# Larger, ordered first transfers and an indexer rotation that swaps halves by DMA, in a two-layer sparse-attention and recurrence trunk

## The chip, the cores and the metric

One core of one Trainium2 chip runs the whole program in one launch. The metric is the device time of that launch in microseconds (us); less is better. The time before is the median of three runs; the profile is of one more execution, with its own time.

## The reference, cut to what matters

Two layers over 256 tokens of width 1024, all in float32. The change touches the indexer, which decides for every query which 64 keys it keeps, and the very first loads.

```
h = rmsnorm(x)
q, k, v, ga, iq, ik, iw, xr, gr, ma, mb = split(h @ w_in)      # iq: 16 heads of 64, ik: one head of 64
iq, ik = rope(iq), rope(ik)          # rope: [x1*c - x2*s, x2*c + x1*s], x1 and x2 the halves (32 + 32)
score[t, s] = sum_h iw[t, h] * relu(iq[t, h] . ik[s])          # causal, the 64 best s per t are kept
attn = softmax over the kept keys (q, k, v);   y_a = (attn * silu(ga)) @ w_out_attn
hr = rg_lru(conv(xr));                         y_b = (hr * silu(gr)) @ w_out_rnn
x = x + (sigmoid(ma)*y_a + sigmoid(mb)*y_b) @ w_o
```

## The kernel before, in words

**Layout.** Activations stand transposed: features on the 128 partitions, the 256 tokens in the free dimension. Every float32 matrix product is made of three fp32r matmuls: weights and activations are each split in a high part (a copy that rounds to fp32r) and a low part (the rest), and high x high, low x high and high x low add up in PSUM. All weights are one stream of 128x128 blocks, eight to a chunk of 512 KB, in the order of use. `Stream` (L528) loads a chunk into `raw` (4 buffers), and makes `wh` by a copy on ACT or DVE (L480, L482) and `wl` by a subtraction on DVE (L486; 6 buffers each). The first two chunks are "halved" (`HALVED`, L1237): they come as four loads of 256 KB into `rah` and become `whh` and `whl`.

**Order of the work.** `plan` (L65) lists the units of a layer: `head` (the indexer's key and weights `pk`, and its first three query blocks `iq`), then the other `iq` blocks, the recurrence (`xr`, `gr`, `gate`), the gates (`ga`, `ma`, `mb`), `q`, `k`, `v` and attention, and the output products. The units record operations; `Program.issue` (L285) then fixes the order on every engine before anything runs. It is a list scheduler: TensorE's work has its place in the units' order as priority, every other operation a due time that is counted back from the matmul that needs it, or from the next user of its buffer (L371). Costs and latencies are constants: a gathering DMA counts 300 ns for each transfer in it, and 2000 ns pass until it has landed (L227, L993). On each engine the instructions then run in exactly that order; one that waits holds up all behind it. All DMAs are issued by one queue, SyncE's (SP).

**The start.** L605 to L620 issue the first loads: half a chunk of weights, `head` (the norm gains, four table columns and the first block of x), the second block of x, more halves and chunks, three pairs of x blocks (`xp`), the positions and the parameters. In the fast memory x is one array in which a partition's eight blocks of 1 KB stand side by side. `scaled` (L766) splits x times the gain into `xg`, high and low; `Norm` sums the squares.

**The indexer.** `head` (L812) and `queries` (L856) rotate. `rotate` (L776) lets ACT copy the PSUM bank to `sw` in pieces of 32 partitions, each from the other half of its group of 64 (four ACT instructions for 128 partitions), while DVE multiplies the PSUM bank by the cosines; two more DVE instructions finish. For a query pair of 128 partitions (two heads of 64) two stacks `iqs` of 128 partitions are then built, each with the high part of one head on 64 partitions and its low part on the other 64, by two copies and two subtractions over 64 partitions each (L860 to L867). For the key, `kh` and `kl` hold the same 64 rows twice, also by two copies and two subtractions. `dots` (L874) multiplies the stacks by `kh` and `kl`; its matmuls get a priority 40 us later than their place (`LATE_DOTS`, L1246). ACT's relu makes `rl`, DVE adds it into the scores `wk`, and `select` (L901) finds the 64 best.

**Buffers that matter.** `iqr`, `sw`, `rl` and other work tiles share the five buffers of `f2`; PSUM has four banks `pp` for projections, two `pq` for dots and logits, two `pt`. `gather` (L978) already moves rows of `xs` between partitions by DMA, for the recurrence's block-diagonal gates, into tiles `xk` and `xf`.

Of the kernel before, what the change touches and what calls it, by code (L numbers as in the profile page):

```python
# [11 lines left out]
F32 = mybir.dt.float32  # L12
# [196 lines left out]
def real(a):  # L209
    return a.ap() if isinstance(a, V) else a  # L210
# [222 lines left out]
def trunk(ctx, tc, xT, pos, pre, par, fgb, wst, out):  # L433
# [15 lines left out]
    def const(s, shape, dt=F32, bufs=1, tag=None):  # L449
        return pg.tile(cp, tag or s, [P] + shape, dt, nm(s), bufs)  # L450

    def r2(s):
        return pg.tile(rp, "r2", [P, 2, T], F32R, nm(s), R2)
# [4 lines left out]
    def f2(s):  # L458
        return pg.tile(fp, "f2", [P, 2, T], F32, nm(s), F2)

    def f1(s):
        return pg.tile(fp, "f1", [P, T], F32, nm(s), F1)
# [2 lines left out]
        return pg.tile(pp, pool, [P, 2, T], F32, nm(s), {"pp": 4, "pq": 2, "pt": 2}[pool])  # L465


    def act(o, i, func, **kw):
        c = (50 if i.psum() else 94) + 0.833 * o.size() + (200 if "accum_out" in kw else 0)
        aps = [kw[k] for k in ("scale", "bias") if isinstance(kw.get(k), V)]  # L470
        outs = [o] + ([kw["accum_out"]] if "accum_out" in kw else [])
        pg.op("act", c + 93 * len(aps), outs, [i] + aps,
              lambda: nc.scalar.activation(real(o), real(i), func, **{k: real(v) for k, v in kw.items()}),
              TABS.get(func))

    def copy(o, i):

        n = o.size()
        pg.op("act", (50 if i.psum() else 94) + 0.833 * n, [o], [i],
              lambda: nc.scalar.activation(real(o), real(i), AF.Copy),  # L480
              alt=(67 + 1.046 * n if i.psum() else 69 + 0.52 * n,
                   lambda: nc.vector.tensor_copy(real(o), real(i))))  # L482
# [11 lines left out]
    def sub(o, a, b):  # L494
        tt(OP.subtract, o, a, b)
# [21 lines left out]
    def load(o, src, cost, beside=False):  # L517

        pg.op("dma", cost, [o], [], lambda: nc.sync.dma_start(real(o), src), beside=beside)
# [8 lines left out]
    class Stream:  # L528
# [6 lines left out]
        def load(self, upto):  # L535
            while self.nload < min(upto, NCH):
                c = self.nload
                self.nload += 1
                if c < HALVED:
                    self.raws[c] = []  # L540
                    for i in range(2):
                        raw = r2f("rah").join()
                        load(raw, wst[c][:, 512 * i:512 * i + 512], 800)
                        self.raws[c].append(raw)
                        yield
                    continue
                raw = pg.tile(wp, "raw", [P, 1024], F32, nm("raw"), RAWS)
                load(raw, wst[c], 1550)
                self.raws[c] = raw
                yield  # L550

        def chunk(self, c):
            if c not in self.parts:
                for _ in self.load(c + 1):
                    pass
                raw = self.raws.pop(c)
                pg.shift = -LEAD
                if c < HALVED:
                    self.parts[c] = []
                    for q in raw:  # L560
                        t = r2("whh").join(), r2("whl").join()
                        split(t, q)
                        self.parts[c].append(t)
                    pg.shift = 0.0
                    return self.parts[c]
                wh = pg.tile(wp, "wh", [P, 1024], F32R, nm("wh"), WBUF)
                wl = pg.tile(wp, "wl", [P, 1024], F32R, nm("wl"), WBUF)
                copy(wh, raw)
                sub(wl, raw, wh.bitcast(F32))
                pg.shift = 0.0  # L570
                self.parts[c] = (wh, wl)
            return self.parts[c]
# [26 lines left out]
    ws = Stream()  # L599
    prm = const("prm", [NPAR - NPRE])  # L600
    head = const("head", [NPRE + 2 * T])
    xp = [head[:, NPRE:].split(2)] + [const(f"xp{i}", [2, T]) for i in range(1, KD // 2)]
    x = [xp[k // 2][:, k % 2, :] for k in range(KD)]
    posi = const("posi", [T], I32)
    first = ws.load(KD // 2)  # L605
    load(head[:, :NPRE + T], pre, 400)
    next(first)
    load(x[1], xT[:, 1, :], 400, True)
    pg.shift = -9000.0
    load(posi, pos, 400)  # L610
    pg.shift = 0.0
    next(first)
    for i in range(1, KD // 2):
        load(xp[i], xT[:, 2 * i:2 * i + 2, :], 800)
        next(first)
        if i < HALVED:
            next(first)
    for _ in first:
        pass
    load(prm, par, 400)  # L620

    def pc(n, i=0):
        i += PC[n]
# [142 lines left out]
    def scaled(l, k):  # L766
# [6 lines left out]
        stt(t[1], xk, g, t[0].bitcast(F32), OP.mult, OP.subtract)  # L773
        return t

    def rotate(o, ps, sw, tabs, step):  # L776

        n = o.shape[0]
        for b in range(0, n, step):
            act(sw[b:b + step], ps[b ^ step:(b ^ step) + step], AF.Copy)  # L780
        mul(o, ps, tabs[0])
        mul(sw, sw, tabs[1])
        add(o, o, sw)
# [4 lines left out]
    class Layer:  # L788
# [23 lines left out]
        def head(self):  # L812

            pk, one, two = bank("pp", "pk"), bank("pp", "iq"), bank("pp", "iq")
            ps = pk[:, 0, :]
            self.R = R = self.norm.finish()
            for k in range(KD):
                for n, o in enumerate((ps, one[:, 0, :], one[:, 1, :], two[:, 0, :])):
                    mm3(o, self.xg[k], k == 0 and n != 2, k == KD - 1, True)
            ci, si = const("ci", [T]), const("si", [T])  # L820
            mul(ci, tab["i"][0], R)
            mul(si, tab["i"][1], R)
            self.ti = (ci, si)
            ikr, iwt = f1("ikr"), f1("iwt")
            rotate(ikr[:64], ps[:64], f1("sw")[:64], [t[:64] for t in self.ti], 32)
            mul(iwt, ps, R)
            kh, kl = self.kh, self.kl
            for b in (0, 64):
                copy(kh[b:b + 64], ikr[:64])
            for b in (0, 64):  # L830
                sub(kl[b:b + 64], ikr[:64], kh.bitcast(F32)[:64])
            pw = bank("pt", "iwps")
            pg.late = LATE_TURN
            for t in range(2):
                trans(pw[:, 0, t * P:t * P + P], iwt[:, t * P:t * P + P])
            pg.late = 0.0
            act(self.iwq, pw[:, 0, :].split(2)[:, :, 64:80], AF.Copy, scale=1.0 / 32.0)
            for k in range(0, KD, 2):
                self.make_h(k)
            self.banks["iq"] = one  # L840
            self.queries(1)
            self.banks["iq"] = two
# [13 lines left out]
        def queries(self, i):  # L856

            iqr = f2("iqr")
            rotate(iqr, self.banks["iq"], f2("sw"), [t.twice() for t in self.ti], 32)
            st = [r2("iqs") for _ in range(2)]  # L860
            for a in range(2):
                s = slice(64 * a, 64 * a + 64)
                copy(st[a][s], iqr[s])
            for a in range(2):
                s = slice(64 * a, 64 * a + 64)
                d = slice(64 - 64 * a, 128 - 64 * a)
                sub(st[a][d], iqr[s], st[a].bitcast(F32)[s])  # L867
            for n in range(2):
                for t in range(2):
                    self.dots(i - 1 + n, [st[a][:, n, :] for a in range(2)], t)  # L870
            if i == 7:
                self.select()
# [105 lines left out]
        def gather(self, kind, rows):  # L978

            parts = stretches(rows)  # L980
            src = {i: self.xs[i] for _, i, _, _ in parts}
            moves = []
            if kind == "plain":
                dst = r2("xf")
                for d, i, a, z in parts:
                    moves.append((dst[d:d + z - a], src[i][a:z]))
            else:
                dst = pg.tile(fp, "f1", [P, T], F32R, nm("xk"), F1)
                for h in range(2):
                    for d, i, a, z in parts:  # L990
                        d += h * len(rows)
                        moves.append((dst[d:d + z - a], src[i][a:z, h, :]))
            pg.op("dma", 300 * len(moves), [dst], list(src.values()),  # L993
                  lambda: [nc.sync.dma_start(real(o.bitcast(F32)), real(i.bitcast(F32))) for o, i in moves][-1])
            return dst

        def gate(self, j):
# [279 lines left out]
def layout(x, positions, norm_g, w_in, conv_w, conv_b, w_rg, b_rg, w_ig, b_ig, lru_lambda, w_out_attn, w_out_rnn,  # L1277
# [4 lines left out]
    def cols(v):  # L1282
        return v.reshape(-1, P).T
# [4 lines left out]
    sgn_a = np.where(p < 64, -1.0, 1.0).astype(np.float32)  # L1288
    sgn_i = np.where(p % 64 < 32, -1.0, 1.0).astype(np.float32)
    cw = conv_w.reshape(L, 4, KR, P).transpose(0, 2, 1, 3)  # L1290
    pre = np.concatenate([cols(norm_g), inv_a[:, None], sgn_a[:, None], inv_i[:, None], sgn_i[:, None], xT[:, 0]], 1)
    assert pre.shape == (P, NPRE + T)
    par = np.concatenate([cols(cw), cols(conv_b), cols(b_rg), cols(b_ig), cols(lru_lambda)], 1)
    assert par.shape == (P, NPAR - NPRE)
    fgb = np.ascontiguousarray(np.broadcast_to(final_g[None, :], (P, D)))
# [25 lines left out]
```

## Time and profile before

| | before |
|---|---|
| median of 3 runs | 707.88 us (706.57 to 708.32) |
| the profiled execution's own time | 706.28 us |
| its span in the profile | 704.5 us |
| TensorE (PE) busy | 687.6 us, 98% |
| VectorE (DVE) busy | 602.8 us, 86% |
| ScalarE (ACT) busy | 478.0 us, 68% |

How to read it: the span is the stretch that the profiler covers, 1.8 us less than the execution's time. A busy share is an average over stages; what an engine could still give is seen in the stretches and in the waits. "a <- b" in a row of instructions means that a is written from b; in brackets stands the idle time of the engine before an instruction and what ended it. For a matmul the time between two starts counts, not its duration, since matmuls overlap.

### The profile page before, as it was taken

The numbers are of one execution on the slowest core, as the hardware profiler recorded it, in microseconds if no ns is written. First come the engines' busy times: TensorE is split into PE (matmuls) and PEld (weight loads), VectorE is DVE, ScalarE is ACT, GpSimd is POOL, SyncE is SP. The second block draws the span as 40 slices with busy tenths as digits, with TensorE's granted clock in tenths as the row PEclk, the third lists the DMA queues.
The fourth block names the chain that finished last, engine by engine and source line by source line (L and its number), as shares of the span: only waits on it lengthen the run. The fifth ranks groups of instructions, "written<-read, shape, count | busy, mean of one in ns | idle before, by whom it ended". The sixth has DMA issues, their size and how long they took to land.

```text
span 704.5 us, 12625 instructions
## 1 busy us (share of the span) xinstructions
PE 687.6 (98%) x4720; PEld 638.4 (91%) x4720; DVE 602.8 (86%) x1179; ACT 478.0 (68%) x771; POOL 6.5 (1%) x18
## 2 busy tenths in 40 slices
PE   6999999999999999999999999999999999999996
PEld 5988999999999998888999899999999898988885
DVE  6989999999898959857779997999989987796573
ACT  7897675798895748544558866588769765773433
POOL 0000000000000000000000000000000000000000
PEclk9999999999999999999999999999999999999999
DMA  8545556666756452655553655566655554535521
GB/s 280 181 155 189 201 187 205 201 205 198 225 176 200 151 182 87 199 172 185 170 180 113 195 192 179 160 222 202 213 207 180 189 182 169 180 98 172 197 73 60
DMA packets 38536, 125.24 MB, mean 178 GB/s; under 512 B 4940, under 2 KB 7564, under 8 KB 38476
## 3 DMA queue, kind: packets, MB, share of 16 engines
q1 hardware_dynamic: 38476, 124.44, 54.1%
q8 instruction: 37, 0.61, 0.3%
q14 instruction: 23, 0.19, 0.1%
HBM read 119.77 MB, written 1.05 MB: 171 GB/s over the span
## 4 chain that ended last, share of the span: by engine, by line
PE 88%; ACT 5%; DVE 3%; issue 2%; DMA 1%; SPq 0%; DVEq 0%
PE rps L512 16%; PE yb L512 9%; PE q L512 7%; PE k L512 7%; PE ops L512 6%; PE ma L512 6%; PE ya L512 6%; PE v L512 6%; PE ga L512 6%; PE mb L512 5%; PE gps L512 5%; PE iq L512 3%; PE dots L512 2%; PE lg L512 2%; PE av L512 2%
## 5 line engine op out<-in xcount | busy, mean ns | idle before, releaser
L486 DVE TENSOR_TENSOR wl<-raw,wh 128x1024 fp32r<-128x1024 f32 x223 | 271.8, 1221 | 57.3 <-ACT wh L480 55.8
L480 ACT ACTIVATE wh<-raw 128x1024 fp32r<-128x1024 f32 x195 | 206.2, 1058 | 142.5 <-PE rps L512 21.9
L512 PE MATMUL rps<-hh,wh 128*128 128x256 f32 x352 | 99.7, 283 | 0.0
L512 PE MATMUL rps<-hl,wh 128*128 128x256 f32 x352 | 99.6, 283 | 0.0
L512 PE MATMUL rps<-hh,wl 128*128 128x256 f32 x352 | 99.6, 283 | 0.0
L512 PEld LDWEIGHTS rps<-hh,wh 128*128 128x128 f32 x352 | 67.4, 192 | 0.6 <-issue 0.4
L512 PEld LDWEIGHTS rps<-hh,wl 128*128 128x128 f32 x352 | 67.4, 191 | 0.2
L512 PEld LDWEIGHTS rps<-hl,wh 128*128 128x128 f32 x352 | 67.4, 191 | 0.0
L512 PE MATMUL yb<-wh,g 128*128 128x512 f32 x176 | 58.9, 396 | 0.0
L512 PE MATMUL iq<-xg,wh 128*128 128x256 f32 x232 | 45.7, 286 | 0.0
L512 PE MATMUL ya<-wh,aT 128*128 128x512 f32 x128 | 40.8, 396 | 0.0
L512 PEld LDWEIGHTS iq<-xg,wh 128*128 128x128 f32 x232 | 37.5, 192 | 0.0
L512 PEld LDWEIGHTS yb<-wh,g 128*128 128x128 f32 x176 | 32.5, 188 | 5.3
L512 PE MATMUL ga<-hh,wh 128*128 128x256 f32 x128 | 36.4, 284 | 0.8 <-DVE iwt L486 0.5
L512 PE MATMUL q<-hh,wl 128*128 128x256 f32 x128 | 36.4, 284 | 0.0
L512 PE MATMUL q<-hh,wh 128*128 128x256 f32 x128 | 36.4, 284 | 0.0
L512 PE MATMUL k<-hh,wl 128*128 128x256 f32 x128 | 36.3, 284 | 0.0
L512 PE MATMUL ga<-hl,wh 128*128 128x256 f32 x128 | 36.3, 283 | 0.0
L512 PE MATMUL q<-hl,wh 128*128 128x256 f32 x128 | 36.2, 283 | 0.0
L512 PE MATMUL k<-hl,wh 128*128 128x256 f32 x128 | 36.2, 283 | 0.0
L512 PE MATMUL k<-hh,wh 128*128 128x256 f32 x128 | 36.2, 283 | 0.0
L512 PE MATMUL ga<-hh,wl 128*128 128x256 f32 x128 | 36.2, 283 | 0.0
(254 smaller groups left out, 1945.4 us busy)
## 6 DMA issues: line engine op xcount, KB each, us to landing
raw<-in_wst_dram SPq DMA_DIRECT2D x223, 512.0 KB, 3.5
xk<-xs SPq DMA_DIRECT2D x24, 48.0 KB, 3.2
rah<-in_wst_dram SPq DMA_DIRECT2D x4, 256.0 KB
out_dram<-z SPq DMA_DIRECT2D x4, 256.0 KB, 2.3
xp<-in_xT_dram SPq DMA_DIRECT2D x3, 256.0 KB
fg<-in_fgb_dram SPq DMA_DIRECT2D x2, 256.0 KB
xk<-xs SPq DMA_DIRECT2D x8, 40.0 KB
xf<-xs SPq DMA_DIRECT2D x2, 160.0 KB
```

The source lines that it names most:

```text
L480: lambda: nc.scalar.activation(real(o), real(i), AF.Copy),
L486: lambda: nc.vector.tensor_tensor(real(o), real(a), real(b), op=op))
L512: lambda: nc.tensor.matmul(real(o), real(w), real(m), start=start, stop=stop, skip_group_check=grp))
```

## The change

It does two things. **First loads:** `head` takes the second block of x too (266 KB in place of 138), the last four blocks of x come as one load of 512 KB (`rest`), and the second weight chunk as one load of 512 KB into `raw`, its halves still being split one by one; only the first chunk is loaded in halves. The loads' order is written out: `head`, the two halves of chunk 0, `xp`, chunk 1, `rest`, chunks 2 and 3, positions, parameters. In memory, the first two blocks of x are part of `pre`, and the other six stand side by side for each partition.

**Rotation:** `rotate32` takes the place of `rotate` for the indexer (q and k of the attention keep the old one). ACT copies the whole bank to `o` in one instruction; a `move` of DMAs, one for each 32 partitions, writes the swapped halves to `sw`; then DVE multiplies `o` and `sw` by the tables and adds. The stacks: one split over all 128 partitions gives `one` (high) and `low`; a move of two DMAs fills `two` with the high and low rows of the second head, and then a move of one DMA overwrites the lower half of `one` with the low rows of the first. For the key, one split of 64 partitions and a move of two DMAs that doubles `kh` and `kl`. In the scheduler a move counts 250 ns for each of its DMAs, and the 2000 ns until it has landed; the existing gather uses the same function, and so counts 250 in place of 300.

```
-                if c < HALVED:
+                if c == 0:
...
-                    for q in raw:
+                    for q in raw if c == 0 else (raw[:, :512], raw[:, 512:]):
...
-    xp = [head[:, NPRE:].split(2)] + [const(f"xp{i}", [2, T]) for i in range(1, KD // 2)]
+    rest = const("xr", [4 * T])
+    xp = [head[:, NPRE:].split(2), const("xp", [2, T]), rest[:, :2 * T].split(2), rest[:, 2 * T:].split(2)]
...
-    load(head[:, :NPRE + T], pre, 400)
-    next(first)
-    load(x[1], xT[:, 1, :], 400, True)
-    pg.shift = -9000.0
-    load(posi, pos, 400)
-    pg.shift = 0.0
-    next(first)
-    for i in range(1, KD // 2):
-        load(xp[i], xT[:, 2 * i:2 * i + 2, :], 800)
-        next(first)
-        if i < HALVED:
-            next(first)
-    for _ in first:
-        pass
-    load(prm, par, 400)
+    def weights():
+        for _ in range(2 if ws.nload == 0 else 1):
+            next(first)
+
+    for n, f in enumerate((lambda: load(head, pre, 800), weights, lambda: load(xp[1].join(), xT[:, :2 * T], 800),
+                           weights, lambda: load(rest, xT[:, 2 * T:], 1550), weights, weights,
+                           lambda: load(posi, pos, 400), lambda: load(prm, par, 400))):
+        pg.shift = -1e6 + 1e4 * n
+        f()
...
+    def move(moves):
+
+        outs, ins = ({a.h: a for a in side}.values() for side in zip(*moves))
+        pg.op("dma", 250 * len(moves), list(outs), list(ins),
+              lambda: [nc.sync.dma_start(real(o.bitcast(F32)), real(i.bitcast(F32))) for o, i in moves][-1])
+
+    def rotate32(o, ps, sw, tabs):
+
+        n = o.shape[0]
+        act(o, ps, AF.Copy, also=(sw,))
+        move([(sw[b:b + 32], o[b ^ 32:(b ^ 32) + 32]) for b in range(0, n, 32)])
+        mul(o, o, tabs[0])
+        mul(sw, sw, tabs[1])
+        add(o, o, sw)
...
-            rotate(ikr[:64], ps[:64], f1("sw")[:64], [t[:64] for t in self.ti], 32)
+            rotate32(ikr[:64], ps[:64], f1("sw")[:64], [t[:64] for t in self.ti])
...
-            for b in (0, 64):
-                copy(kh[b:b + 64], ikr[:64])
-            for b in (0, 64):
-                sub(kl[b:b + 64], ikr[:64], kh.bitcast(F32)[:64])
+            split((kh[:64], kl[:64]), ikr[:64])
+            move([(t[64:], t[:64]) for t in (kh, kl)])
...
-            rotate(iqr, self.banks["iq"], f2("sw"), [t.twice() for t in self.ti], 32)
-            st = [r2("iqs") for _ in range(2)]
-            for a in range(2):
-                s = slice(64 * a, 64 * a + 64)
-                copy(st[a][s], iqr[s])
-            for a in range(2):
-                s = slice(64 * a, 64 * a + 64)
-                d = slice(64 - 64 * a, 128 - 64 * a)
-                sub(st[a][d], iqr[s], st[a].bitcast(F32)[s])
+            rotate32(iqr, self.banks["iq"], f2("sw"), [t.twice() for t in self.ti])
+            one, low, two = r2("iqs"), r2("iql"), r2("iqs")
+            split((one, low), iqr)
+            move([(two[:64], one[64:]), (two[64:], low[64:])])
+            move([(one[64:], low[:64])])
+            st = one, two
...
-            pg.op("dma", 300 * len(moves), [dst], list(src.values()),
-                  lambda: [nc.sync.dma_start(real(o.bitcast(F32)), real(i.bitcast(F32))) for o, i in moves][-1])
+            move(moves)
```

## Rows read from the trace of the kernel before

**Rows 1.** The page: busy time of each engine over the span.
```profile
PE 687.6 (98%) x4720; PEld 638.4 (91%) x4720; DVE 602.8 (86%) x1179; ACT 478.0 (68%) x771; POOL 6.5 (1%) x18
```

**Rows 2.** Busy time by stretch: PE, PEld, DVE, ACT, POOL, clock, DMA share, GB/s.
```profile
0.00:5.00 5.00, 0.16 (x1) 0.16 (x1) 0.76 (x4) 2.51 (x4) 1.28 (x10) 1.00 0.58 124
5.00:9.00 4.00, 3.85 (x15) 3.22 (x16) 1.71 (x5) 2.17 (x4) 0.00 (x0) 1.00 0.86 279
9.00:12.00 3.00, 2.95 (x23) 2.58 (x22) 2.65 (x6) 2.35 (x4) 0.00 (x0) 1.00 1.05 412
12.00:16.00 4.00, 2.34 (x17) 2.14 (x18) 3.96 (x8) 4.00 (x9) 0.00 (x0) 1.00 1.04 396
20.00:62.00 42.00, 39.00 (x292) 36.59 (x293) 38.50 (x63) 37.26 (x56) 0.00 (x0) 1.00 0.52 167
62.00:375.00 313.00, 313.00 (x2191) 292.98 (x2190) 273.16 (x559) 210.46 (x341) 2.65 (x4) 1.00 0.57 184
400.00:440.00 40.00, 38.89 (x300) 37.36 (x299) 35.93 (x71) 25.26 (x44) 0.32 (x1) 1.00 0.61 193
440.00:680.00 240.00, 240.00 (x1588) 220.31 (x1587) 206.95 (x411) 159.51 (x261) 2.27 (x4) 1.00 0.55 179
```

**Rows 3.** Who PE waited for over the whole span: total us, times, longest.
```profile
PE mb L512 <- DVE ga L486: 1.3, 1, 1.3
PE dots L512 <- ACT rl L473: 1.1, 1, 1.1
...
PE dots L512 <- DVE kl L486: 0.8, 1, 0.8
...
PE ga L512 <- DVE iwt L486: 0.5, 1, 0.5
```

**Rows 4.** Timeline, first 16 us: start, duration, instruction, idle before it.
```profile
4.84 0.58 PE L512 MATMUL pk<-xg,whh 128*128 128x256 f32 x1 [4.84 <-ACT xg L771]
...
5.71 0.51 ACT L771 ACTIVATE xg<-head 128x256 fp32r<-128x256 f32 x1 [0.92 <-DMA head<-in_xT_dram]
...
7.28 0.63 ACT L480 ACTIVATE whh<-rah 128x512 fp32r<-128x512 f32 x1 [1.06 <-DMA rah<-in_wst_dram]
...
14.27 0.38 PE L512 MATMUL pk<-xg,whl 128*128 128x256 f32 x1 [0.94 <-DVE whl L486]
...
15.44 0.28 PE L512 MATMUL pk<-xg,wh 128*128 128x256 f32 x1
...
15.56 0.28 PE L512 MATMUL pk<-xg,wl 128*128 128x256 f32 x1
```

**Rows 5.** ACT's instructions in 20 to 80 us by form: count, busy us, mean ns.
```profile
L473 ACT ACTIVATE sw<-iq 32x512 f32<-32x512 f32 x16 | 9.4, 590 | 0.3
L480 ACT ACTIVATE iqs<-iqr 64x512 fp32r<-64x512 f32 x7 | 4.4, 629 | 0.2
...
L480 ACT ACTIVATE kh<-ikr 64x256 fp32r<-64x256 f32 x2 | 0.8, 418 | 1.1 <-DVE ikr L486 1.1
```

**Rows 6.** DVE's instructions in 20 to 80 us by form.
```profile
L486 DVE TENSOR_TENSOR iqs<-iqr,iqs 64x512 fp32r<-64x512 f32 x8 | 5.5, 686 | 3.3 <-ACT iqs L480 3.1
...
L486 DVE TENSOR_TENSOR kl<-ikr,kh 64x256 fp32r<-64x256 f32 x2 | 0.8, 416 | 0.0
```

**Rows 7.** Timeline: the last query block's last matmul, its bank's product, `kl`'s last subtraction.
```profile
44.08 0.28 PE L512 MATMUL iq<-xg,wh 128*128 128x256 f32 x1
...
56.39 0.68 DVE L486 TENSOR_TENSOR iqr<-iq,ci 128x512 f32<-128x512 f32 x1
...
60.03 0.42 DVE L486 TENSOR_TENSOR kl<-ikr,kh 64x256 fp32r<-64x256 f32 x1
```

**Rows 8.** The tile `xk` of the existing gather: issue ns min/median/max, and landing.
```profile
L994 SPq DMA_DIRECT2D xk<-xs x64: 519/586/1311, 77.1 to 518.4; - x64
...
DMA to landing us min/median/max: 3.0/3.2/3.4
```

**Rows 9.** What the DMA queue (SP) waited for, 20 to 110 us.
```profile
SPq L519 <- DVE wl L486: 59.3, 22, 4.8
```

More of the change, by code (lines that the diff above doesn't have):

```diff
@@ L465, in bank, with act @@
         return pg.tile(pp, pool, [P, 2, T], F32, nm(s), {"pp": 4, "pq": 2, "pt": 2}[pool])
-    def act(o, i, func, **kw):
+    def act(o, i, func, also=(), **kw):
         c = (50 if i.psum() else 94) + 0.833 * o.size() + (200 if "accum_out" in kw else 0)
         aps = [kw[k] for k in ("scale", "bias") if isinstance(kw.get(k), V)]
-        outs = [o] + ([kw["accum_out"]] if "accum_out" in kw else [])
+        outs = [o, *also] + ([kw["accum_out"]] if "accum_out" in kw else [])
         pg.op("act", c + 93 * len(aps), outs, [i] + aps,
@@ L1290, in layout @@
     cw = conv_w.reshape(L, 4, KR, P).transpose(0, 2, 1, 3)
-    pre = np.concatenate([cols(norm_g), inv_a[:, None], sgn_a[:, None], inv_i[:, None], sgn_i[:, None], xT[:, 0]], 1)
-    assert pre.shape == (P, NPRE + T)
+    pre = np.concatenate([cols(norm_g), inv_a[:, None], sgn_a[:, None], inv_i[:, None], sgn_i[:, None],
+                          xT[:, 0], xT[:, 1]], 1)
+    assert pre.shape == (P, NPRE + 2 * T)
+    xT = np.ascontiguousarray(xT[:, 2:].reshape(P, -1))
     par = np.concatenate([cols(cw), cols(conv_b), cols(b_rg), cols(b_ig), cols(lru_lambda)], 1)
```

## Prediction

> **What bounds the kernel now.** I read the busy shares first: TensorE is busy for 687.6 of 704.5 us [rows 1], so at most 16.9 us can be won without removing a matmul, and this change removes none. The stretches say where they lie [rows 2]: 4.8 us before the first matmul, 0.15 + 0.05 + 1.66 up to 16 us, 3.0 between 20 and 62, 1.1 between 400 and 440, and the rest behind the last matmul, where nothing changes. From 62 to 375 us and from 440 to 680 PE is never idle, so whatever arrives earlier at 62 us arrives earlier at the end. One loss is hidden in the busy time: 5 to 9 us has 15 matmuls in 3.85 us, against 23 in 2.95 in the next stretch, though the granted clock reads 1.00, the upper of its two levels of 1.2 and 2.4 GHz, in both [rows 2]. So the first ones run at about half the rate after an engine that had done nothing; I take that as fixed, and only moved with the first matmul.
>
> Then I asked who ends PE's waits. Before 16 us it is late data: ACT, which makes PE's operands, itself waits 0.92 us for the second x block and 1.06 for the second weight half [rows 4]. Between 20 and 62 us it is two engines that are both nearly full, DVE 38.5 and ACT 37.3 of 42 us [rows 2]: `mb` waits 1.3 us for a bank that DVE's `ga` frees, `ga` 0.5 for one that `iwt` frees, `dots` 0.8 for `kl` [rows 3]. In the second layer `dots` waits 1.1 us for `rl` [rows 3].
>
> **The change, part by part.**
>
> *A, the first loads.* Before, the bytes moved were 0.62 MB by 5 us, 1.74 by 9 and 2.97 by 12 (GB/s times length of the first three stretches [rows 2]). The new order has `head` and the first weight half, 0.53 MB, ahead of the first matmul, where before it was 0.40 (256 + 138 KB). On that curve the 0.13 MB more cost 0.5 to 1 us; but both loads were of rows of about 1 or 2 KB among other small ones, and the rate at the start is only 124 GB/s against 412 later, so larger rows may buy it back. I put the first matmul at 5.2 us, 0.4 late. What follows is better fed: the second x block is in `head`, the second half follows at once (0.80 MB in all), `xp` makes 1.06, chunk 1 1.58, `rest` 2.11, chunk 2 2.63 MB, on the curve at about 8.4, 9.9 and 11.2 us for the last three. Before, PE reached the first matmul of chunk 2 at 15.44 [rows 4]. The 48 matmuls until there take 5.8 us at full rate (a start every 0.12 us, 15.44 to 15.56 [rows 4]); from 5.2, with some 18 at half rate (2.2 us more) and 0.6 for a wait on the split of chunk 1 or 2, that is 13.8: a gain of 1.6. Bounds: a loss of 1.0, if the first two loads land late and nothing is recovered (14.27 shows that PE then waits for `whl`, not data [rows 4]); a gain of 3, if PE starts at 4.8 and waits for nothing. I take 1.6, as ACT's two waits on DMA (2.0 us together [rows 4]) are the nearest rows.
>
> *B, what ACT and DVE lose.* Per query pair: four ACT copies of 590 ns become one, two high copies of 629 ns become one, two low subtractions of 686 ns become one [rows 5, 6]. That is 1.77 + 0.63 = 2.4 us of ACT and 0.69 of DVE. For the key: one copy of 418 ns and one shorter still less on ACT, one subtraction of 416 on DVE. With four pairs a layer: ACT some 10 us (4 x 2.4 and the key's) and DVE 3.2 us less per layer. The multiplications stay at three per rotation; the first now reads SBUF, which the others here do at the same length. Nearly all of it falls in 20 to 80 us, where DVE was full; with ACT freed, copies that the scheduler gave DVE can go back too. The PSUM banks come free sooner: the last query pair's bank was held until DVE's product at 57.1 us [rows 7], 13 us after its matmuls; now one ACT copy frees it. Of the 3.0 us that PE stood idle from 20 to 62 [rows 2], the wait for `kl` with its restart is about 1.0; the other 2.0 hang on banks and operands that ACT or DVE gave late (`ga` and `iwt` are 1.8 of them by name [rows 3]). Their bounds are 2.0 and, if DVE stays the last to finish, 0; I take 1.9, since the banks' release is what the change takes from DVE. In the second layer I take 0.5 of the 1.1, bounds 0 and 1.1.
>
> *C, what the moves add.* Seven DMAs per query pair, four per layer for the key: 32 issues a layer at 586 ns [rows 8], 18.8 us of SP. SP waits most of the time for a free `raw` buffer (59.3 us in 22 waits [rows 9]), so the issues hide; without that cover they would be 18.8 us late for weights. Bytes: 640 KB per pair, some 2.8 MB a layer in about 50 us, 56 GB/s on top of 167, below the 412 seen: hidden. Behind a move that waits for ACT or DVE stand weight loads; they run up to four chunks ahead, 11 us of matmuls, so a wait of 1 to 3 us is covered too.
>
> The latency is not so clearly covered. No query row exists for it; the nearest is the gather's: 3.2 us to landing and 0.59 per issue. The swap of four then takes 3 x 0.59 + 3.2 = 5.0 us where the scheduler counts 4 x 0.25 + 2.0 = 3.0; a move of two 3.8 for 2.5, of one 3.2 for 2.25. DVE is in order: if the multiplication behind a swap was placed just where the swap was thought to land, DVE stands still for 2.0 us, and weights' `wl` wait behind it, and PE for them. Against that: the copy is due early (its bank is needed), the product late (its dots run 40 us later), so between them other work lies; I cost it at nothing. The last hops are nearer to PE: before, `kl` was finished at 60.45, and PE was waiting [rows 3, 7]. With it placed just in time again, the doubling lands 1.3 us later than counted. I take 0.8 us, for both layers together, between 0 and 1.3 for each of four (two keys, two last pairs), 5.2.
>
> By the Trainium skill, page "DMA: Bandwidth & Descriptors", section "Anatomy of one DMA", a DMA costs a constant 2.0 us plus its bytes at 436 GB/s. By that 64 KB would take an estimated 2.15 us, and the last hops would cost nothing, 0.8 us less in the sum. The gather's rows disagree: its 48 KB took 3.2 us [rows 8].
>
> *Sum.* 1.6 + 1.9 + 0.5 - 0.8 = **3.2 us less**: 704.5 to 701.3 in span, 706.28 to 703.1 in this execution's time. The median of the runs is 1.6 us above the profiled one, so the median should go from 707.88 to **704.7**.
>
> **The rivals.** What a measurement here can tell from no change is about 0.3%, 2.1 us.
>
> *Absorbed.* The start moves 1 us at most, because the first matmul now waits for two larger loads and DVE, 3.96 of 4 us busy from 12 on [rows 2], sets the pace to 62 us; the waits on `mb` and `ga` shrink, those on `dots` grow by as much. For it: DVE is busy 38.5 of 42 us [rows 2], and the change takes only 3.2 from it. Against: ACT's waits at the start were on DMA, not DVE. Bounds' middle: 0.5 + 1.0 + 0.2 - 0.8, about 0.9 less: 707.0.
>
> *Slower: DVE stands at the swap.* The multiplications are placed at the counted landing of the swaps, and each stalls DVE 2.0 us (key: 1.3). In layer 0 that is 4 x 2.0 + 1.3 = 9.3 us of idle DVE against 3.2 saved, in a stretch where DVE has nothing to spare: PE loses 6, the start gives 1.6 back, layer 1 costs nothing more as it had 0.5 us in hand: about 4 slower, 712. It decides once the stalls exceed 3.2 + 1.6 us a layer, more than two of four swaps. For it: the difference of 2 us is certain by [rows 8]. Against: before, the product at 56.39 came 12 us after its matmuls [rows 7], so DVE takes these late, when the swap has long landed.
>
> *First loads do not help.* The first matmul comes at 6 us and chunk 2 no earlier than 15.4: A is -0.5, the rest as forecast, 1.1 less: 706.8. This joins "absorbed" in the chances.
>
> **How the numbers follow.** Forecast 0.53; absorbed, or no help at the start, 0.28; slower 0.19. Faster by over 0.3% is the forecast alone, 0.53. The low end gives the forecast the rest of the bounds, A 1.4, B 0.1 + 0.6, C 0.8, and 0.8 for the spread of the runs, 3.7 below it: 701.0. The high end takes in "absorbed" and most of "slower", up to 711.0. The likeliest case's own range is 701.0 to 705.7.
>
> **What would show it.** Right: the first matmul by 5.5 us, the first one of chunk 2 before 14.5, no ACT wait on `xp` or `rah` above 0.5 us; ACT 10 us less busy in 20 to 80 us; PE busy over 40.5 of the 42 us from 20 to 62; no DVE wait on `sw`. Moves landing in 3 to 3.5 us. Wrong: DVE or PE idle before `iqr`, `sw` or `dots`, released by DMA; ACT's `wh` waiting for `raw` behind a move on SP; a first matmul after 6 us.

## The result, and the profile of the changed kernel

The changed kernel takes **712.5 us** (median of 4 runs, 712.1 to 714.7) where the kernel before, run beside it, takes 708.0 (706.6 to 708.3): a ratio of 1.0086 (1.0073 to 1.0098). It is slower, where 704.7 was forecast. The profiled run took 712.52 us with a span of 710.7, 6.2 us longer than before.

Where the time went is read from the stretches, against [rows 2] (PE, PEld, DVE, ACT, POOL, granted clock, DMA share, GB/s):

```profile
0.00:5.00 5.00, 0.00 (x0) 0.00 (x0) 1.66 (x6) 2.94 (x5) 1.28 (x10) 1.00 0.59 176
5.00:9.00 4.00, 3.87 (x17) 3.85 (x18) 3.02 (x7) 2.92 (x7) 0.00 (x0) 1.00 0.98 380
12.00:16.00 4.00, 4.00 (x36) 4.00 (x36) 4.00 (x9) 3.97 (x7) 0.00 (x0) 1.00 0.73 278
20.00:62.00 42.00, 36.35 (x274) 34.56 (x273) 35.23 (x66) 26.24 (x36) 0.00 (x0) 0.99 0.69 211
400.00:440.00 40.00, 35.90 (x257) 34.10 (x257) 31.98 (x60) 22.47 (x38) 0.00 (x0) 0.96 0.67 199
...
62.00:64.00 2.00, 2.00 (x11) 2.00 (x11) 1.19 (x3) 0.98 (x2) 0.00 (x0) 0.50 0.93 355
...
62.00:100.00 38.00, 37.84 (x280) 36.04 (x280) 35.95 (x78) 27.04 (x47) 0.29 (x1) 0.96 0.73 212
```

The start is better: 4.00 us of matmuls in 12 to 16 us against 2.34. ACT and DVE are relieved: in 20 to 62 us ACT falls from 37.3 to 26.2 us, DVE from 38.5 to 35.2, though part of that is work that has not come yet, as the stretch holds 18 matmuls fewer. And yet PE loses there: 5.65 us idle against 3.0, and in the second layer 4.1 against 1.1. Behind the longest holes the clock drops (0.50 at 62 to 64 us is the 1.2 GHz level); as means of 0.96 over 38 and 40 us that is an estimated 1.5 + 1.6 us more. Together 2.65 + 3.0 + 3.1 lost and 2.2 gained at the start (below) is 6.5, against 6.2 measured.

The page's busy line shows the same contradiction, against [rows 1]: ACT works 19 us less and DVE 7, and the kernel is longer.

```profile
PE 689.4 (97%) x4720; PEld 641.4 (90%) x4720; DVE 595.4 (84%) x1166; ACT 458.9 (65%) x738; POOL 5.9 (1%) x18
```

Who PE waited for over the span of the changed kernel, against [rows 3]:

```profile
PE pk L512 <- ACT whh L480: 5.1, 1, 5.1
PE dots L512 <- ACT rl L473: 4.1, 2, 2.7
PE dots L512 <- DMA kh<-kh: 3.7, 1, 3.7
PE mb L512 <- ACT iqr L473: 1.9, 1, 1.9
```

The first line is the start, where PE waits for the first weight half; behind it not one names weights. To see why `kh`, `iqr` and `rl` are late one has to go back to ACT and the queue. First who ACT waited for, 20 to 100 us and then 365 to 425 us (before, they were two in 365 to 430 us, 1.2 us together, and none from 20 to 100):

```profile
ACT wh L480 <- DMA raw<-in_wst_dram: 10.0, 4, 5.7
...
ACT wh L480 <- DMA raw<-in_wst_dram: 8.1, 5, 2.4
```

Then the timelines of the changed kernel: the queue (SP), then ACT, DVE and PE in the first layer (start, duration, instruction, idle before it and what ended that):

```profile
26.41 0.53 SPq L519 DMA_DIRECT2D raw<-in_wst_dram  x1
30.68 2.41 SPq L777 DMA_DIRECT2D sw<-iqr  x4
33.13 11.36 SPq L519 DMA_DIRECT2D raw<-in_wst_dram  x7
...
37.48 1.06 ACT L480 ACTIVATE wh<-raw 128x1024 fp32r<-128x1024 f32 x1 [5.75 <-DMA raw<-in_wst_dram]
...
38.57 1.23 DVE L486 TENSOR_TENSOR wl<-raw,wh 128x1024 fp32r<-128x1024 f32 x1 [3.26 <-ACT wh L480]
...
44.19 0.51 ACT L687 ACTIVATE stab_i<-ang,head 128x256 f32<-128x256 f32 x1
...
48.46 2.41 SPq L777 DMA_DIRECT2D sw<-iqr  x4
...
53.90 0.69 DVE L486 TENSOR_TENSOR iqr<-iqr,ci 128x512 f32<-128x512 f32 x1 [2.54 <-DMA sw<-iqr]
54.51 0.41 DVE L486 TENSOR_TENSOR ikr<-ikr,sw 64x256 f32<-64x256 f32 x1
...
56.59 0.41 DVE L486 TENSOR_TENSOR kl<-ikr,kh 64x256 fp32r<-64x256 f32 x1
...
57.08 0.49 SPq L777 DMA_DIRECT2D kh<-kh  x1
...
61.18 0.36 PE L512 MATMUL dots<-kh,iqs 128*128 128x256 f32 x1 [3.69 <-DMA kh<-kh]
```

Read it downwards. After the load at 26.41 SP stands in front of a swap, whose data ACT has only at 30.66 (SP's waits put 3.4 us of this down to DVE's `hl` and 0.3 to ACT's `iqr`), and issues the next weight load at 33.13. ACT, in order, stands 5.75 us at the `wh` of a chunk that PE doesn't need yet (PE is busy without a gap from 20 to 40 us). DVE stands behind it at `wl`, with the last steps of the sine tables queued behind. The sines run at 44.19, the rotation after them. Then DVE stands 2.54 us at a swap that was itself issued late, at 48.46, with the key's last rotation step (54.51) behind it, and the key's halves reach PE 3.7 us late. In the second layer there is no table, but `rl` stands behind `wh` in the same way: five waits for `raw` in a row between 394 and 409 us, with PE waiting for `rl` behind them.

```profile
401.69 1.06 ACT L480 ACTIVATE wh<-raw 128x1024 fp32r<-128x1024 f32 x1 [1.44 <-DMA raw<-in_wst_dram]
405.11 1.06 ACT L480 ACTIVATE wh<-raw 128x1024 fp32r<-128x1024 f32 x1 [2.36 <-DMA raw<-in_wst_dram]
...
406.65 0.37 ACT L473 ACTIVATE rl<-dots 128x256 f32<-128x256 f32 x1
408.13 1.06 ACT L480 ACTIVATE wh<-raw 128x1024 fp32r<-128x1024 f32 x1 [1.11 <-DMA raw<-in_wst_dram]
409.09 0.58 ACT L473 ACTIVATE rl<-dots 128x512 f32<-128x512 f32 x1
...
407.07 0.39 PE L512 MATMUL dots<-kh,iqs 128*128 128x256 f32 x1 [2.67 <-ACT rl L473]
```

The scheduler that fixed these orders believed in something else. It counts 250 ns for each DMA of a move, and its plan (worked out when the kernel is built) puts the load behind that swap at 28.7 us, the key's doubling at 50.4; the trace has them at 33.13 and 57.08. Each DMA of a move takes SP 584 ns (median; the two lines are the swaps' issues, and the landing of all tiles called `sw`):

```profile
L777 SPq DMA_DIRECT2D sw<-iqr x32: 507/584/603, 22.6 to 400.3; - x32
...
DMA to landing us min/median/max: 1.9/2.7/5.2
```

By the Trainium skill, page "DMA: Bandwidth & Descriptors", section "Anatomy of one DMA", the DMA engines don't wait on semaphores; the issuing sequencer does, before it dispatches. The trace agrees: SP's hold before 30.68 is 3.7 us of waits on instructions of DVE and ACT, and no load behind it starts.

### The profile page after: what moved, and what is told of

It reads as the page before. It is cut to its first block, busy times and chain, and to the rows that moved or that the text cites. A ratio compares the mean times of both kernels' runs of the same rounds, so it can differ in the third digit from the quotient of the medians.

```text
span 710.7 us, 12704 instructions
## 1 busy us (share of the span) xinstructions
PE 689.4 (97%) x4720; PEld 641.4 (90%) x4720; DVE 595.4 (84%) x1166; ACT 458.9 (65%) x738; POOL 5.9 (1%) x18
## 4 chain that ended last, share of the span: by engine, by line
PE 87%; DMA 6%; ACT 2%; DVE 2%; issue 1%; SPq 1%; DVEq 0%; ACTq 0%
PE rps L512 15%; PE yb L512 9%; PE q L512 6%; PE k L512 6%; PE ops L512 6%; PE ma L512 6%; PE ya L512 6%; PE v L512 6%; PE ga L512 6%; PE mb L512 5%; PE gps L512 5%; PE iq L512 3%; DMA raw<-in_wst_dram 2%; PE dots L512 2%; DMA iqs<-iql 2%; PE lg L512 2%
```

## The experiments

All times are medians in us, the ratio is to the kernel before on the same chip, with its interval. "Booked" is what the scheduler counts for a move of n DMAs; the existing gather stays at 250 ns in all of them.

**1. The two parts apart.** One kernel has the new first loads and the old rotation, one the old loads and the new rotation.

```
e1:  rotate32(...), split, move   ->  rotate(...), copy, copy, sub, sub     (as before)
e2:  head/xp/rest, weights()      ->  the loads of before
```

> The new first loads with the old rotation and stacks (the gather counts 300 ns again). All theories put the loss into the rotation: the first matmul of chunk 2 near 13.3 us as in the changed kernel, no idle PE beyond 3 us from 20 to 62, total 704.5 to 706.5 us, 2 to 3 us under the kernel before. If the loads themselves cost something later (a schedule that shifts), it would be at 708 or more.

> The new rotation and stacks with the old first loads. If the two parts simply add, this is 712.5 plus the 2.2 us that the loads gave: 714.5 to 715.5 us. If the loss needs the earlier start (the tables come late because the positions are loaded last), it is under 711 us.

Loads only: 706.13 (0.9997, 0.9988 to 1.0005). Rotation only: 710.62 (1.0071, 1.0056 to 1.0087). The loss is the rotation's. The parts don't add, though: with the new loads on top it was 712.5, not less. The expectation's sign for a loss that needs the earlier start, a time under 711, came true by 0.4 us; as the two intervals overlap, this decides nothing. In the rotation-only kernel ACT's longest wait for `raw` in 20 to 100 us is only 1.2 us. PE stands 3.9 us there for a stack whose last move SP issued at 48.37 (planned for 43.43), behind a swap and the key's two doublings (SP and PE of the rotation-only kernel):

```profile
44.39 2.65 SPq L780 DMA_DIRECT2D sw<-iqr  x4
47.14 0.54 SPq L780 DMA_DIRECT2D kh<-kh  x1
47.77 0.54 SPq L780 DMA_DIRECT2D kl<-kl  x1
48.37 0.59 SPq L780 DMA_DIRECT2D iqs<-iql  x1
...
50.87 0.55 PE L512 MATMUL dots<-kh,iqs 128*128 128x256 f32 x1 [3.91 <-DMA iqs<-iql]
```

So moves are late behind moves, too, without a long wait at `wh`.

The loads alone gain nothing although chunk 2 starts 2.8 us earlier, at 12.62; PE gives it back at the next bank that DVE has to free, and then runs slow (PE of the loads-only kernel; the last line is its stretch 32 to 34 us):

```profile
31.42 0.36 PE L512 MATMUL ga<-hh,wh 128*128 128x256 f32 x1 [2.49 <-DVE iwt L486]
...
32.00:34.00 2.00, 2.00 (x13) 2.00 (x12) 2.00 (x3) 1.95 (x4) 0.00 (x0) 0.53 0.00 0
```

**2. The rotation's two halves.** Swaps by DMA with the old stacks, and stacks by DMA with ACT's old rotation, both still booked at 250 ns.

```
e8:  split + move of the stacks and of kh, kl  ->  copy, copy, sub, sub
e9:  rotate32(...)                             ->  rotate(..., 32)
```

> The changed kernel with the swap by DMA but stacks and key halves built by ACT and DVE as before; 250 ns for each DMA. If the last hops before PE (kh, the second half of the stacks) make the loss, PE has no wait for a DMA here: 704 to 708 us. If the swap's placement on DVE makes it (2 us for each of four), PE still waits behind kl and rl: 709 to 713.

> The changed kernel with the stacks and key halves by DMA, the rotation by ACT's four copies as before; 250 ns for each DMA. The swap alone took 710.5. If the last hops before PE are placed wrong by themselves, PE waits for kh or iqs and the time is 707 to 712; if only the swap's place is wrong, 703 to 706.5.

Swap only 710.50 (1.0056, 1.0039 to 1.0072); stacks only 713.33 (1.0092, 1.0078 to 1.0107). Either half alone loses. With swaps only, ACT's longest wait for `raw` is 6.6 us. With stacks only it is 2.2, yet PE waits 4.5 us for `kh`; there SP itself stood up to 5.3 us behind one move with the others behind it, and PE 3.6 us for a bank of the old rotation, as in the loads-only kernel. So a long wait at one `wh` isn't needed for the loss.

**3. Another queue.** The moves issue on GpSimd's queue; the planned orders are the same.

```
-              lambda: [nc.sync.dma_start(...) ...
+              lambda: [nc.gpsimd.dma_start(...) ...
```

> The changed kernel with the rotation's moves issued by GpSimd's queue in place of SyncE's; order and planned times are the same. Queue theory (moves that wait hold up the weight loads behind them on SP): ACT's waits for raw, 10.0 us in 20 to 100 and 8.1 in 365 to 425, fall under 4 us each, and the total falls by 3 to 6 us, to 706.5 to 709.5. Latency theory (the hops land later than the scheduler counts): GpSimd's moves land no sooner, so PE and DVE wait at kh, sw and dots as before or longer: 711.5 to 715.

709.72 (1.0049, 1.0037 to 1.0061): 2.8 us better than the change, not cured, and between what the two theories had expected. SP now issues loads and no move of the rotation, and ACT still waits 9.7 us for `raw` in 20 to 100 us, 4.4 at the longest: the loads wait for buffers that DVE frees (SP waits 53.2 us for `wl` between 14 and 90 us). That already speaks against SP's issues alone. The moves land later, too, but SP's own land as late in experiments 6 and 7 (medians of 4.7 and 4.5 us), so this isn't shown to be the queue's doing (both from the page's list of DMA issues: KB, us to landing; the changed kernel, then this one):

```profile
sw<-iqr SPq DMA_DIRECT2D x32, 64.0 KB, 2.4
```

```profile
sw<-iqr POOLq DMA_DIRECT2D x32, 64.0 KB, 4.0
```

**4. What the scheduler believes.** The kernel's work and its DMAs are those of the change; only the constant is another, and the orders that follow from it. First everywhere, and the same with the old loads:

```
e4:  move(): 250 * n  ->  590 * n + 1000        e7: the same, with the loads of before
```

> The changed kernel, the scheduler told the measured duration of the rotation's moves (590 ns for each DMA in place of 250, and 1.0 us more until landing). Latency theory: the waits for sw (2.5 us on DVE) and kh (3.7 us on PE) go, PE stands idle under 3 us from 40 to 70, total 706 to 709. Queue theory: moves still stand in SP's queue before weight loads; ACT's waits for raw stay above 6 us per layer, total 710.5 to 714.

> The old first loads with the new rotation and the measured duration in the scheduler. The loads gave 2.2 us at the start but nothing alone, since PE then waited 2.5 us for the bank that iwt and the tables hold, and ran 4 us at half the clock after that. With the rotation by DMA that wait is gone in the changed kernel. If the two parts need each other, this is 703 to 704.5 us, 2 to 3 above the run with both; if the loads are worth nothing also here, 701 to 702.

701.35 (0.9925, 0.9913 to 0.9937) and 702.99 (0.9951, 0.9938 to 0.9964). Both theories as put there were missed: 706 to 709 was expected if the late landing costs, 710.5 to 714 if the queue does. 11 us come from one constant, and the first loads are now worth 1.6. A constant does three things, which the next four kernels take apart: it moves the due times of what comes ahead of the move, it occupies the queue, and it puts the move's consumers later.

```
e5:   due times 590n + 1000, queue and consumers 250n
e6:   queue and consumers 590n + 1000, due times 250n
e13:  queue 250n, consumers 340n + 1000 later, due times 250n
e12:  queue 590n + 1000, consumers as early as with 250n, due times 250n
```

> The changed kernel; the scheduler uses the measured duration of a move only where it counts due times backwards, and 250 ns for each DMA where it places the next instruction. The run told the measured duration everywhere took 701.4 us. If the gain lies in starting the chain earlier, this one is at 701 to 704; if it lies in not placing DVE's and PE's next instruction before the data is there, this one stays at 709 to 713 with waits for sw and kh as in the changed kernel.

> The other half: due times counted with 250 ns for each DMA, the next instruction placed by the measured duration. If the placing is what matters, 701 to 704.5 us and no wait of PE for kh; if the early start matters, dots come late in the plan too, and PE stands behind ACT's rl or in the plan's own gaps: 707 to 712.

> The other half: SP's queue booked at 250 ns for each DMA, the consumers placed by the measured landing. If the consumers' place is what matters, 699 to 702 us, no PE wait for a DMA, though ACT may wait longer for raw; if the queue's booking matters, 706 to 712.

> The run with due times of 250 ns and placing by the measured duration took 699.4 us. Here the scheduler books SP's queue for the measured duration, but thinks the data landed as early as in the changed kernel. If the loss comes from weight loads that stand behind moves on a queue booked too short, this keeps the gain: 699 to 702 us. If it comes from DVE and PE placed before the data is there, it stays near the changed kernel, 708 to 713, with PE waiting for kh or iqs.

Due times only 713.09 (1.0088, 1.0071 to 1.0105); queue and consumers 699.35 (0.9900, 0.9885 to 0.9914); consumers only 712.95 (1.0084, 1.0070 to 1.0098); **queue only 698.40** (0.9882, 0.9869 to 0.9896), the fastest of all and faster than both kernels. Only the booking of the queue counts. Consumers that wait for the landing gain nothing, so it isn't what costs that the plan underrates the landing of the moves, which was the prediction's worry. The fast one's stretches and its ACT wait, 20 to 100 us:

```profile
20.00:62.00 42.00, 41.68 (x319) 40.04 (x319) 40.27 (x81) 27.63 (x43) 0.00 (x0) 1.00 0.76 216
400.00:440.00 40.00, 40.00 (x301) 38.28 (x301) 37.66 (x80) 24.60 (x41) 1.91 (x2) 1.00 0.72 222
...
ACT wh L482 <- DMA raw<-in_wst_dram: 5.2, 3, 2.4
```

PE loses 0.3 us in the two stretches together, and its clock reads 1.00 in both. The tables run at 40.11 there, 4 us earlier, because one `wl` fewer stands ahead of them on DVE.

**5. A third dose.** Queue booked with the issue time alone. (In the expectations from here on, theory Q is that weight loads are stuck behind waiting moves in SP's queue, and rival P that the longer booking merely led to another order of ACT and DVE.)

```
e15:  as e12, 590 * n + 1000  ->  590 * n
```

> As the run that only books the queue, but with 590 ns for each DMA of a move and without the 1000 ns on top; landing as early as in the changed kernel. Theory Q: most of the gain follows from booking the issue time alone, 698 to 703. Rival P (luck of one order): anywhere between 698 and 713, with no link to ACT's longest wait for raw; Q wants that wait under 3 us if the time is under 703, and over 4 if it is over 709.

709.29 (1.0034, 1.0021 to 1.0047; 11 runs, 706.4 to 710.9). Between the two, and well above the 698 to 703 that were expected: the issue time alone isn't enough. ACT's longest wait for `raw` was 3.8 us, where theory Q wanted over 4 with a time above 709. The 1000 ns on top were first put in as a longer landing (e4). That on the queue they cover what SP spends waiting in front of a move is a reading, not shown; the value was a guess, and which waits it has to cover was not taken apart.

**6. SP's order alone.** Here the orders of PE, ACT, DVE and GpSimd stay the changed kernel's, instruction for instruction; seven swaps move behind one to three weight loads each.

```
-        for o in sorted(order, key=lambda o: (o.start, o.no)):
+        for o in sorted(order, key=lambda o: (o.end + 1900.0 if o.swap else o.start, o.no)):
```

> The changed kernel with one thing altered: in SP's order each swap stands behind the weight loads that the plan places within the time the swap was thought to land (one to three loads). The orders of PE, ACT, DVE and GpSimd are the changed kernel's, instruction for instruction; seven swaps move in SP's. Theory Q (weight loads stuck behind waiting swaps): ACT's longest wait for raw falls from 5.7 us to under 3, PE's waits for dots and mb shrink, and the time falls by at least 6 us, to 706 or less. Rival P (booking the queue longer helped because it made the scheduler arrange ACT and DVE otherwise): those orders are unchanged, so the time stays within 2 us of 712.5, and as the swaps now land later, DVE waits for sw.

**714.33** (1.0110, 1.0097 to 1.0123): a clear miss for theory Q as put there, while both signs of rival P came true: within 2 us of 712.5, and DVE waiting for `sw`. ACT's longest wait for `raw` did fall, from 5.7 to 3.2 us, but there are five in place of four, 11.5 us in all, and the sines run at 45.24. SP has the same ten DMAs to issue between the same loads, so the loads are late in three steps instead of one; and the swaps that were moved back came late, too: DVE waited 4.8 us for one, and PE's wait at `dots` became 6.3 us. So the place of a load in the queue is not what is wrong; what is left is that ACT and DVE follow an order made for loads and moves that can't be there.

**7. Slack in place of booking.** The copy out of the bank took from the tables and the rotation what made them urgent: the sines run at 44.19 us where before they ran at 28.85. Theory S: that lost slack is the cause.

```
e17:  sine and cosine tables due 15 us earlier              (booked 250n)
e18:  and rotation, splits and moves due 8 us earlier       (booked 250n)
e19:  as e18, queue booked as in e12
```

> The changed kernel, moves still booked at 250 ns, with one thing altered: the operations that make the indexer's sine and cosine tables are due 15 us earlier. In the plan the tables move from 37.6 to 25.8 us and the doubling of the key lands some 6 us ahead of the first dots instead of 0.4. Theory S (the copy out of the bank took away what made the tables and the rotation urgent, so the plan puts them just in time, and any wait on the queue becomes a wait of PE): the sines run near 29 us instead of 44.2, PE's waits for kh and mb in the first layer go (5.6 us and the low clock behind them), the second layer, which makes no such tables, keeps its loss: 706 to 709. Theory Q (weight loads stand behind moves in SP's queue, which only a longer booking cures): 711 or more, with ACT still waiting over 5 us for raw.

> As the run with early tables, and the rotation, the splits and the moves of the key and of every query pair are due 8 us earlier too, in both layers; moves booked at 250 ns. Theory S: the second layer gains as well, 699 to 703, without any change of the queue's booking. Theory Q: 709 or more.

> Both cures at once: the queue booked at 590 ns for each DMA and 1000 on top, and tables and rotation due 15 and 8 us earlier. If both cure the same loss, they don't add up: 697 to 700, as the booking alone gave 698.4. If they cure different losses, it is under 697.

Tables early 708.65 (1.0023, 1.0006 to 1.0039; 12 runs, 704.5 to 711.4); all early **716.06** (1.0131, 1.0117 to 1.0146); all early and booked 700.25 (0.9916, 0.9904 to 0.9928). The first fits theory S in part: in 20 to 62 us PE idles 2.4 us in place of 5.65 and the wait for `mb` is gone, but 1.6 us at `kh` and a mean clock of 0.96 are left. The second refutes it: with the most slack the kernel is the slowest, as the moves come in a heap and SP issues nine of them, but one weight load, between 45.6 and 52.4 us (SP, ACT and PE of the all-early kernel):

```profile
45.56 2.44 SPq L779 DMA_DIRECT2D sw<-iqr  x4
48.11 0.54 SPq L779 DMA_DIRECT2D iqs<-iql  x1
48.74 0.53 SPq L519 DMA_DIRECT2D raw<-in_wst_dram  x1
49.33 0.49 SPq L779 DMA_DIRECT2D kh<-kh  x1
...
52.47 0.99 SPq L519 DMA_DIRECT2D raw<-in_wst_dram  x2
...
54.92 1.06 ACT L480 ACTIVATE wh<-raw 128x1024 fp32r<-128x1024 f32 x1 [6.43 <-DMA raw<-in_wst_dram]
...
63.33 0.58 PE L512 MATMUL dots<-kh,iqs 128*128 128x256 f32 x1 [5.69 <-ACT rl L473]
```

The same slack with the queue booked takes 700.25, 15.8 us less, and 1.9 more than the booking alone: slack doesn't add to it.

**8. Booking for the other forms.** Stacks only, booked; and both stacks filled by one move of four into fresh tiles, which takes away the wait of the second move on the first.

```
e16:  as e9, queue booked as in e12
e10:  as e6, move([(d[h:h+64], t[64*a:64*a+64]) for h, t in ((0, high), (64, low)) for a, d in ...])
```

> The stacks and the key's halves by DMA, the old rotation on ACT, and the queue booked with 590 ns for each DMA and 1000 on top. The same with 250 ns took 713.33. Theory Q (SP's order also delays the stacks and the key's halves): PE's waits for kh (4.5 us) go, 700 to 706. Rival: the stacks by DMA are slow in themselves, their hops end too late for the dots however they are planned: 710 or more.

> The run of 699.4 us with one change: both stacks are filled by one move of four DMAs into fresh tiles, so that SP no longer waits for the first move to land before it issues the second. If SP's waiting there still costs something, 697.5 to 699; if it is covered, 699 to 700.5, and SP's waits for iqs are gone without effect.

Stacks only, booked: 703.63 (0.9956, 0.9944 to 0.9968), against 713.33; PE's wait for `kh` is gone. One move: 699.75 (0.9901, 0.9887 to 0.9915) against 699.35 for its like: the wait between the two moves costs nothing once it is booked.

All kernels with moves on SP, with ACT's waits for `raw` (20 to 100 and 365 to 430 us together; 1.2 us before):

| queue booked | kernels | time | ACT waits for `raw`, us |
|---|---|---|---|
| 250n | change; e2, e5, e8, e9, e13, e14, e17, e18 | 708.65 to 716.06, none faster than before | 8.1 to 20.7 |
| 590n | e15 | 709.29 | 12.9 |
| 590n + 1000 | e4, e6, e7, e10, e12, e16, e19 | 698.40 to 703.63, all faster than before | 2.2 to 11.4 |

The last column overlaps: 8.1 us went with a slower kernel (e2), 11.4 with a faster one (e10), so the sum of these waits is no measure of the loss. What does part the groups is how far the trace is from the plan. Counted load by load, the weight loads that a kernel's own scheduler puts between 22 and 62 us are issued on average 4.1 to 8.4 us later than planned in the kernels booked at 250n, 2.6 in e15, and from 1.8 us earlier to 2.8 later in those with 590n + 1000. But in the kernel before they are 5.8 us late as well, and PE idles only 3.0 us there, so lateness by itself is not the loss either.

Shown is that in these 17 kernels the booking of the queue decides the sign, and that neither due times, nor consumers, nor slack, nor SP's order of swaps does. That it works by placing `wh` and `wl` where their loads really are is read from the traces; no run fixes the orders of ACT and DVE by hand, and that link is argued. Nor do the runs part loads that are late behind moves from moves that are late behind moves: the booking changes both at once.

## Why the prediction was wrong, point by point

**A, the first loads: right, and somewhat more.** First matmul at 5.13 us (5.2 forecast), the first one of chunk 2 at 13.25 against 15.44 [rows 4], 2.2 us earlier (1.6 forecast). Of ACT's two early waits for data the one for the second x block is gone and 0.40 of the 1.06 us for the second weight half is left; 0.68 us for `xp` is new, above the 0.5 that the signs allowed:

```profile
5.13 0.58 PE L512 MATMUL pk<-xg,whh 128*128 128x256 f32 x1 [5.13 <-ACT whh L480]
...
13.25 0.28 PE L512 MATMUL pk<-xg,wh 128*128 128x256 f32 x1
```

The half rate of the first matmuls was not "only moved with the first matmul", as the prediction took it: starts every 0.21 us lasted to 8.7 us before and to 10.1 here, and with the same loads to 8.2 in the loads-only and 9.4 in the queue-only kernel. Chunk 2 starts in that order, at 12.62, 12.86 and 13.25, so a spread of some 0.6 us in this gain is not the loads' doing.

But "whatever arrives earlier at 62 us arrives earlier at the end" passes over the banks between: alone the loads are worth nothing that can be measured (0.3 us), with a rotation that frees the bank and a booked queue 1.6.

**B, the relief: right in the work, and right in its worth where nothing hides it.** Over the span ACT works 19.1 us less and DVE 7.4, which is 9.6 and 3.7 a layer (10 and 3.2 forecast). With the queue booked PE idles 0.3 us there in place of 3.0, so the relief is worth 2.7, not 1.9, and 1.1 in the second layer, not 0.5.

**C, the moves: here the step failed.** The words are "the issues hide" and "Behind a move that waits for ACT or DVE stand weight loads; they run up to four chunks ahead, 11 us of matmuls, so a wait of 1 to 3 us is covered too". The issue time was right (584 ns against 586), and so was the cover for PE: after the first matmul it never waited for weights. But a weight load isn't handed to PE. It goes through `wh` on ACT and `wl` on DVE, which run in order and have the tables, `iqs` and `rl` queued behind; those have no four chunks of cover. The question that was asked of DVE, who is queued behind the waiting instruction, was not asked of ACT at `wh`. Nor was it asked of the moves: on SP they stand behind one another, too, with no cover at all (experiments 1 and 2). The price was 5.65 + 4.1 us of idle PE in place of the 3.0 + 1.1 of before and some 3 us of low clock.

The term that was priced, 0.8 us for last hops that land late, is not what costs: putting the consumers later (712.95) leaves all the loss in place. The landing is not one number. The gather's row gave 3.2 us [rows 8]; swaps of 64 KB took 2.4 on the page of the changed kernel and 2.7 over all `sw`, but 2.0 to 4.7 in the other kernels with moves on SP. The prediction set the row against a figure of the Trainium skill, page "DMA: Bandwidth & Descriptors", section "Anatomy of one DMA — SWDGE (gpsimd) path", and left out that the section gives it for DMAs issued by GpSimd, where SP issued these; an estimate by it for 64 KB is 2.15 us. The trace of moves that GpSimd issued doesn't agree: they took 4.0 us (experiment 3).

**The rivals.** "Slower: DVE stands at the swap" gave 712 and was held for 0.19. Its time came out by luck, for its mechanism came true in a small part only: DVE waited for `sw` once between 20 and 100 us, 2.5 us, where 9.3 were reckoned. There the swap took 5.4 us from its first issue (48.46) to the multiplication (53.90), near the 5.0 reckoned, and this wait is on the way to PE's hole at 61.18; but it came once and not at each swap, and placing the consumers later didn't help (e13). "Absorbed" fell: the time rose, and with the queue booked PE idles only 0.3 us in 20 to 62 us although DVE is busy for 40.3 of the 42. The list of signs did name the true one, "ACT's `wh` waiting for `raw` behind a move on SP", but no rival was built on it. The end of the range at 711.0 missed by 1.5 us, as it took in only most of the slower case.

Without the failed step the terms hold: in the queue-only kernel the span is 696.8 us, 7.7 less than before; chunk 2 starts 2.6 earlier there (12.86), and the two stretches give 2.7 and 1.1. That is 6.4; the other 1.3 was not assigned.

## What to carry to other kernels

A queue that issues in order is an engine like any other: a scheduler that fixes orders ahead should book for each transfer more than a guess of its issue, or it will place work on other engines behind data that can't be there; here that one constant was worth 14 us of 712, and the issue time alone was not enough. When a change puts transfers on a queue that also brings weights, follow a late weight through the engine that converts it, and ask what stands behind it there, rather than how many chunks the matmul engine has in hand. And when moving things in the queue doesn't help, look at the orders that were made with the wrong price.

## What the runs showed of the hardware that was not expected

- The time lost is more than the idle time. After PE had stood 3.69 us, the granted clock from 62 to 64 us was 0.50, the 1.2 GHz level, and matmuls of 128x256 started every 0.21 us where they start every 0.12 otherwise. The loads-only kernel shows the same behind 2.49 us (0.53 from 32 to 34 us). Behind the 1.86 us before `mb` at 48.49 the clock stayed at 1.00.
- The same 64 KB between partitions, issued by SP, landed after a median of 2.0 to 2.9 us in nine of the kernels, but after 4.7 where the swaps stood behind weight loads (e14) and 4.5 where the moves came in a heap (e18). The 4.0 us of GpSimd's queue lie within that spread; what sets the landing was not taken apart.
